# A diffusion layer on one core: products of the down-projection added up in PSUM, half sums on VectorE, a reordered end

## The chip, the cores and the metric

The kernel runs on one core of a Trainium2 chip. A core has five engines that matter here: TensorE (PE, with its weight loads PEld), VectorE (DVE), ScalarE (ACT), GpSimd (POOL) and SyncE (SP, which issues the DMAs). Each works through its own list of instructions in order and waits for others by semaphores. The metric is device time in microseconds, the median of three runs: 1337.65 us (1335.8 to 1337.68).

## The reference

One layer of a diffusion backbone over 1024 latent tokens and 256 context tokens, width 1024, all in float32: a token mixer (linear recurrence beside attention), then a gated convolution FFN with 2816 hidden channels, each wrapped in norms and modulation. The part that matters here is the last matmul of the FFN and what stands behind it:

```
def conv_ffn(h, w_up, conv_w, conv_b, w_down):
    up = dwconv(h @ w_up, conv_w, conv_b, FFN_CONV_LEFT)
    u, g = up[..., :D_FF], up[..., D_FF:]
    return (jax.nn.silu(g) * u) @ w_down
...
        x = x + gt2 * rms_norm(f_l, g_post_ffn[l])
```

`silu(g) * u` is called act here: 2816 channels by 1024 tokens. The down-projection is act (as 1024 x 2816) times w_down (2816 x 1024).

## The kernel before

The kernel is one long program for one core; in this part the order of every engine's work is the order of the code. The up-projection comes first; its results go through the convolution and the gate and into a buffer in DRAM, act_d, in 22 pages of 128 channels.

The down-projection, from 1100 us on, uses seven block products in place of eight. Both matrices are cut in halves along the 2816 channels (11 blocks of 128 each, NK = 11), act also into its left and right 512 tokens, w_down into its left and right 512 columns. A page of 128 x 1024 holds in its left half (lh) a piece of act and in its right half (rh) a piece of w_down; `ld` loads four kinds of page, blk[1] to blk[4]. A product n, numbered 1 to 7, works for each of its 11 blocks j on such a page or on one whose halves are sums of two pages' halves. `sums` makes these half sums (128 x 512 each), `prep` cuts the page into a high part (ScalarE's copy to the narrower float32r) and a low part (VectorE's difference, through the helper `lo`, line 76), and `dn` multiplies: for four tiles t of 128 tokens, three matmuls high x high, high x low, low x high, each 128 x 128 by 128 x 512.

A product and a block make a slot, 66 slots for the first six products in ORDER. In slot s the code issues the matmuls of s, the half sums for slot s + 4 and the parts for slot s + 3. Every product sums its 11 blocks in four PSUM banks of its own (`bank` hands out eight in turn), and `dn_out` takes the banks out in the first four slots of the following product: a copy on ScalarE or an add on VectorE into the result pages yt[0] to yt[7]. `dn_sums` adds pages once more. GpSimd does one half sum in each block of products 7, 5, 6, 3 and 4, VectorE the other one in products 7, 5 and 6.

Product 2 comes last and in three parts: tiles 0 and 1 together, then tile 2, then tile 3. The upper result pages yt[4] to yt[7] are complete before it and are finished beside it, by `fin`: a square with a row sum on ScalarE, the product with the row gt2, one over the root of the mean by a chain of small instructions (`rstd_of`, lines 101 to 106), then a scaling and addition on VectorE (line 1640) and the store. Pages yt[0] to yt[3] wait for product 2; `fin_head` does the half of their work that can be done early.

Pages come from a list `free`, from which `take` takes the oldest and to which `give` returns; a page is only written when its last reader has ended.

Of the kernel before, what the change touches and what calls it, by code (L numbers as in the profile page):

```python
# [14 lines left out]
D = 1024  # L15
# [6 lines left out]
EPS = 1e-6  # L22
# [12 lines left out]
def hybrid_layer_kernel(ctx: ExitStack, tc: tile.TileContext, A, out):  # L35
    nc = tc.nc
    V, S, G, T = nc.vector, nc.scalar, nc.gpsimd, nc.tensor
# [233 lines left out]
    junk = C([128, 384], mybir.dt.bfloat16)  # L271
# [77 lines left out]
    for n in range(4, 16):  # L349
        b, kp = order[n]  # L350
# [345 lines left out]
    for k in range(2):  # L696
# [3 lines left out]
        h_, l_ = L(F32R), L(F32R)  # L700
# [621 lines left out]
    free = []  # L1322

    def take(dt=F32R):
        k = free.pop(0)
        return {"L": L, "W": W, "F": Fp}[k](dt), k

    def give(*pages):
        free.extend(k for _, k in pages)

    blk = {c: {} for c in (1, 2, 3, 4)}
    opd = {}
    sm = {}
    dpo = {}
    yt = {}

# [6 lines left out]
        for e in es:  # L1343
            nc.sync.dma_start(out=blk[c][j][0][:, rh if e else lh], in_=(A["w_dn"] if e else act_d)[r:r + 128, x])

    def tt(e, o, a, b, op):
        (V if e == "v" else G).tensor_tensor(o, a, b, op)

    def sums(n, j):

        b = {c: blk[c][j][0] for c in blk if j in blk[c]}
        if n == 5:
            tt("g", b[2][:, lh], b[2][:, lh], b[3][:, lh], ALU.add)
            tt("v", b[2][:, rh], b[2][:, rh], b[1][:, rh], ALU.subtract)
        elif n == 6:
            tt("g", b[2][:, lh], b[2][:, lh], b[1][:, lh], ALU.subtract)
            tt("v", b[2][:, rh], b[3][:, rh], b[2][:, rh], ALU.subtract)
            give(blk[1].pop(j))
        elif n == 7:
            x = sm[j] = take(F32)  # L1360
            tt("g", x[0][:, lh], b[1][:, lh], b[2][:, lh], ALU.subtract)
            tt("v", x[0][:, rh], b[3][:, rh], b[2][:, rh], ALU.subtract)
        elif n == 3:
            tt("g", b[2][:, lh], b[4][:, lh], b[2][:, lh], ALU.subtract)
        elif n == 4:
            tt("g", b[2][:, rh], b[2][:, rh], b[4][:, rh], ALU.subtract)

    def prep(n, j):

        hi, l_ = take(), take()  # L1370
        if n in (3, 4):
            for p, x in ((blk[2][j], lh), (blk[3][j], rh)) if n == 3 else ((blk[3][j], lh), (blk[2][j], rh)):
                S.activation(hi[0][:, x], p[0][:, x], AF.Copy)
                lo("v", l_[0][:, x], p[0][:, x], hi[0][:, x])
        else:
            src = sm[j] if n == 7 else blk[{1: 1, 5: 2, 6: 2, 2: 4}[n]][j]
            S.activation(hi[0], src[0], AF.Copy)
            lo("v", l_[0], src[0], hi[0])
        if n == 7:
            give(sm.pop(j))  # L1380
        elif n == 2:
            give(blk[4].pop(j))
        elif n == 4:
            give(blk[2].pop(j), blk[3].pop(j))
        opd[n, j] = hi, l_

    def dn(n, j, ts=(0, 1, 2, 3)):
        hi, l_ = opd[n, j][0][0], opd[n, j][1][0]
        for t in ts:
            if j == 0:  # L1390
                dpo[n, t] = bank(t % 2)
            po = dpo[n, t]
            c = slice(t * 128, (t + 1) * 128)
            T.matmul(po, hi[:, c], hi[:, rh], start=j == 0, stop=False)
            T.matmul(po, hi[:, c], l_[:, rh], start=False, stop=False)  # L1395
            T.matmul(po, l_[:, c], hi[:, rh], start=False, stop=j == NK - 1)
        if 3 in ts:
            give(*opd.pop((n, j)))

    def dn_out(n, t):  # L1400

        po = dpo.pop((n, t))
        if n == 1:
            yt[t] = take(F32)[0]
        if n == 7:
            yt[4 + t] = take(F32)[0]
        y0, y1 = yt[t], yt.get(4 + t)
        if n in (1, 7, 5):
            S.activation(y0[:, lh] if n == 1 else y1[:, lh] if n == 7 else y1[:, rh], po, AF.Copy)
        elif n == 6:  # L1410
            V.tensor_tensor(y0[:, rh], po, y0[:, lh], ALU.add)
        elif n == 3:
            V.tensor_tensor(y0[:, rh], po, y0[:, rh], ALU.add)
        elif n == 4:
            V.tensor_tensor(y1[:, lh], y1[:, lh], po, ALU.subtract)
        else:
            V.tensor_tensor(y0[:, lh], po, y0[:, lh], ALU.add)  # L1417

    def dn_sums(t, q):

        y0, y1 = yt[t], yt[4 + t]
        if q == 0:
            G.tensor_tensor(y1[:, lh], y1[:, lh], y0[:, rh], ALU.add)
            V.tensor_tensor(y0[:, rh], y0[:, rh], y1[:, rh], ALU.add)
        else:
            G.tensor_tensor(y1[:, rh], y1[:, rh], y1[:, lh], ALU.add)

    with tc.manual_schedule():

# [149 lines left out]
            xo[i] = take(F32)[0]  # L1579
            nc.sync.dma_start(out=xo[i], in_=x1_d[i * 128:(i + 1) * 128, :])  # L1580

        ORDER = (1, 7, 5, 6, 3, 4, 2)
        slots = [(n, j) for n in ORDER[:-1] for j in range(NK)]
        preps = [(n, j) for n in ORDER[:-1] for j in range(NK)][3:]
        preps2 = list(range(NK))
        for s_, (n, j) in enumerate(slots):
            q = s_ // NK
            dn(n, j)
            if q and j < 4:
                dn_out(ORDER[q - 1], j)  # L1590
            if n == 1:
                if tail:
                    tail.pop(0)()
                for k in (2 * j, 2 * j + 1) if j < 4 else (j + 4,) if j < 7 else ():
                    ld(2, k)
                    ld(3, k, (1,))
            elif n == 7:
                ld(3, j, (0,))
            elif n == 6:
                ld(4, j)  # L1600
            elif n == 3:
                if 1 <= j < 5:
                    dn_sums(j - 1, 0)
                elif 5 <= j < 9:
                    dn_sums(j - 5, 1)
# [11 lines left out]
        ssf, rsf, epf = C([128, 8]), C([128, 8]), C([128, 8])
        yg = {}

        def fin_head(i):  # L1620


            c = slice(i, i + 1)
            yg[i] = take(F32)[0]
            S.activation(yg[i][:, rh], yt[i][:, rh], AF.Square, accum_out=ssf[:, c])
            V.tensor_scalar(out=epf[:, c], in0=ssf[:, c], scalar1=1.0 / D, scalar2=EPS, op0=ALU.mult, op1=ALU.add)
            G.tensor_tensor(yg[i][:, rh], yt[i][:, rh], gt2[:, rh], ALU.mult)

        def fin(i):

            c = slice(i, i + 1)
            a = lh if i < 4 else slice(0, D)
            if i >= 4:
                yg[i] = take(F32)[0]
            junk, k = take(F32)
            S.activation(junk[:, a], yt[i][:, a], AF.Square, accum_out=ssf[:, c])  # L1636
            (V if i < 4 else G).tensor_tensor(yg[i][:, a], yt[i][:, a], gt2[:, a], ALU.mult)
            rstd_of(rsf[:, c], ssf[:, c], 1, 1.0 / D, epf[:, c] if i < 4 else EPS)
            for a in (lh, rh):
                V.scalar_tensor_tensor(out=xo[i][:, a], in0=yg[i][:, a], scalar=rsf[:, c], in1=xo[i][:, a], op0=ALU.mult, op1=ALU.add)  # L1640
                nc.sync.dma_start(out=out[i * 128:(i + 1) * 128, a], in_=xo[i][:, a])
            free.append(k)

        for j in range(NK):
            dn(2, j, (0, 1))
            if preps2:
                prep(2, preps2.pop(0))
            if j < 4:
                x1_load(j)
                dn_out(4, j)  # L1650
            if j >= 3 and j < 11 and j % 2:
                fin(4 + (j - 3) // 2)
            elif j >= 3 and j < 11:
                fin_head((j - 4) // 2)
        dn_out(2, 0)
        fin(0)
        for j in range(NK):
            dn(2, j, (2,))
        dn_out(2, 1)
        fin(1)  # L1660
        for j in range(NK):
            dn(2, j, (3,))
        for t in (2, 3):
            dn_out(2, t)
            fin(t)
    pe_ctx.close()
    pe_r.close()

# [86 lines left out]
```

## Time and profile before

| what | value |
|---|---|
| median of the runs | 1337.65 us |
| profiled execution | 1337.59 us, span 1335.70 us |
| TensorE busy | 1279.3 us (96%) |
| VectorE busy | 1059.3 us (79%) |
| ScalarE busy | 730.3 us (55%) |
| GpSimd busy | 524.3 us (39%) |
| mean granted TensorE clock | 0.986 of full |
| down-projection, first to last matmul start | 1100.47 to 1321.23 us |

The span runs from the first to the last instruction. A row of a timeline gives when an instruction (or xN merged ones) started and how long it shows; neighbouring instructions on an engine overlap a little, so the step from one start to the next is shorter than what a row shows. Matmuls are pipelined: one shows 0.39 us, but the next starts after less.

### The profile page before, as it was taken

To read this page: it belongs to the slowest core of one execution; us is meant where nothing else is said; L and a number is where in the kernel's file an instruction comes from. 1 tells how busy PE (TensorE), PEld (TensorE's weight loads), DVE (VectorE), ACT (ScalarE), POOL (GpSimd) and SP (SyncE) were. 2 spreads that over 40 slices of the span, in tenths; PEclk is the share of its full clock that TensorE was granted. 3 is DMA by queue.
4 is the path that set the end of the run, shared out by engine and by line. 5 is a ranking of instruction groups with operands and counts; after the bars stand their busy time and mean duration, and the time that the engine had idled before them with its cause. 6 is when DMAs were issued, how large, how long until landed. Compare 5 with 4: busy or idle time off the path is not lost. (4 is left out here: it accounts for less than half of the span.)

```text
span 1335.7 us, 18049 instructions
## 1 busy us (share of the span) xinstructions
PE 1279.3 (96%) x6490; PEld 1049.6 (79%) x6490; DVE 1059.3 (79%) x1633; ACT 730.3 (55%) x1366; POOL 524.3 (39%) x441
## 2 busy tenths in 40 slices
PE   5999999799999999999998999999999999999895
PEld 3796666687999999888776888888888888878684
DVE  3654677768898988847589888887778779998998
ACT  4533785458999999934355433344334435334362
POOL 2410000215666666723042344423442324873922
PEclk8999999899999999999998999999999999999998
DMA  9533244000000001333321222222222368031033
GB/s 372 197 111 127 86 143 130 12 1 1 1 1 1 1 1 49 111 126 140 129 95 48 95 95 86 72 79 95 91 68 78 111 204 316 1 110 64 16 137 115
DMA packets 42184, 124.21 MB, mean 93 GB/s; under 512 B 4696, under 2 KB 4976, under 8 KB 42096
## 3 DMA queue, kind: packets, MB, share of 16 engines
q1 hardware_dynamic: 42096, 123.07, 26.2%
q8 instruction: 51, 0.84, 0.3%
q14 instruction: 37, 0.30, 0.1%
HBM read 101.02 MB, written 22.03 MB: 92 GB/s over the span
## 5 line engine op out<-in xcount | busy, mean ns | idle before, releaser
L1217 PE MATMUL b<-l,f 128*128 128x512 f32 x620 | 242.6, 391 | 5.6 <-DVE f L76 5.6
L1216 PE MATMUL b<-l,f 128*128 128x512 f32 x620 | 242.9, 392 | 3.9 <-DVE l L76 3.8
L1215 PE MATMUL b<-l,f 128*128 128x512 f32 x620 | 242.4, 391 | 0.5 <-issue 0.5
L1217 PEld LDWEIGHTS b<-l,f 128*128 128x128 f32 x620 | 117.0, 189 | 30.7 <-DVE f L76 6.4
L1216 PEld LDWEIGHTS b<-l,f 128*128 128x128 f32 x620 | 116.9, 189 | 30.5 <-DVE l L76 6.5
L906 POOL TENSOR_SCALAR r<-r,c 128x512 f32<-128x512 f32 (+1 forms) x128 | 100.9, 800 | 97.2 <-DVE c L901 68.2
L1215 PEld LDWEIGHTS b<-l,f 128*128 128x128 f32 x620 | 117.0, 189 | 25.2 <-issue 0.7
L1190 ACT ACTIVATE f<-w 128x1024 fp32r<-128x1024 f32 x21 | 22.3, 1060 | 198.8 <-POOL w L1187 198.8
L883 DVE TENSOR_REDUCE c<-s 128x1 f32<-128x512 f32 (+1 forms) x192 | 108.6, 594 | 25.6 <-PE s L880 24.1
L76 DVE TENSOR_TENSOR f<-w,f 128x1024 fp32r<-128x1024 f32 (+1 forms) x89 | 97.1, 1093 | 33.9 <-ACT f L1190 32.9
L1274 DVE SCALAR_TENSOR_TENSOR l<-f,c,l 128x1023 f32<-128x1023 f32 x88 | 123.4, 1403 | 0.7
L894 ACT ACTIVATE r<-s,c 128x512 f32<-128x512 f32 (+1 forms) x192 | 117.5, 620 | 6.2 <-DVE c L901 4.7
L1184 POOL TENSOR_TENSOR w<-w 128x512 f32<-128x512 f32 x21 | 27.9, 1328 | 230.7 <-DVE f L76 230.7
L76 DVE TENSOR_TENSOR l<-t,l 128x512 fp32r<-128x512 f32 x128 | 81.5, 678 | 1.4 <-ACT l L69 1.2
L914 PE MATMUL t<-c,r 128*128 128x128 f32 x640 | 81.7, 273 | 0.9 <-DVE r L76 0.6
L69 ACT ACTIVATE l<-t 128x512 fp32r<-128x512 f32 x128 | 69.4, 595 | 8.5 <-PE t L914 7.7
L1268 ACT ACTIVATE l<-f,c 128x1024 f32<-128x1024 f32 x44 | 54.5, 1238 | 34.9 <-DVE f L1255 34.4
L914 PEld LDWEIGHTS t<-c,r 128*128 128x128 f32 x640 | 71.3, 140 | 2.6 <-PE t L914 0.8
L878 PE MATMUL s<-r,w 96*128 96x512 f32 (+1 forms) x192 | 69.5, 362 | 1.0 <-ACT r L894 0.7
L1063 PE MATMUL po<-l,r 128*128 128x512 f32 x256 | 69.3, 390 | 0.0
L938 PE MATMUL o<-l,r 128*128 128x256 f32 x256 | 68.7, 301 | 0.0
L879 PE MATMUL s<-r,w 96*128 96x512 f32 (+1 forms) x192 | 68.6, 358 | 0.0
(376 smaller groups left out, 3318.2 us busy)
## 6 DMA issues: line engine op xcount, KB each, us to landing
w<-in_w_up SPq DMA_DIRECT2D x44, 512.0 KB
r<-in_w_mod SPq DMA_DIRECT2D x32, 512.0 KB
act<-l SPq DMA_DIRECT2D x22, 512.0 KB
l<-in_w_m SPq DMA_DIRECT2D x16, 512.0 KB
l<-act SPq DMA_DIRECT2D x30, 256.0 KB
l<-in_w_dn SPq DMA_DIRECT2D x30, 256.0 KB
w<-in_w_fm SPq DMA_DIRECT2D x8, 512.0 KB
w<-in_w_out SPq DMA_DIRECT2D x8, 512.0 KB
```

The lines of the kernel that those rows point to most:

```text
L69: S.activation(o, i, AF.Copy)
L76: return (V if e == "v" else G).tensor_tensor(o, src, f(hi), ALU.subtract)
L878: T.matmul(ps[:, :n], qh[0:96, q], kh[0:96, a:a + n], start=True, stop=False)
L883: V.tensor_reduce(out=stat[:, i % 4, c:c + 1], in_=sc[i, c][:, :CK[c][1]], op=ALU.min, axis=AX.X)
L894: S.activation(pt_[i][:, a:a + n], sc.pop((i, c))[:, :n], AF.Exp, scale=-1.0, bias=st[:, 3:4], accum_out=st[:, 4 + c:5 + c])
L906: G.tensor_scalar(out=p[:, a:a + n], in0=p[:, a:a + n], scalar1=stat[:, i % 4, 7:8], scalar2=1.0, op0=ALU.mult, op1=ALU.mult)
L914: T.transpose(ps[:, c, :], pt_[i][:, (c0 + c) * 128:(c0 + c + 1) * 128], ident)
L1063: T.matmul(po[:, n * 512:(n + 1) * 512], w, wo[k][0][:, n * 512:(n + 1) * 512], start=st, stop=en)
L1215: T.matmul(po, wh, bh, start=k == 0 and b == wb[0][1], stop=False)
L1216: T.matmul(po, wh, bl, start=False, stop=False)
L1217: T.matmul(po, wl, bh, start=False, stop=k == 3 and b == wb[-1][1])
L1274: V.scalar_tensor_tensor(out=x[:, a], in0=x0[:, b], scalar=P("fcw", j * 3 + k, 1), in1=x[:, a], op0=ALU.mult, op1=ALU.add)
```

## The change

Products that belong to the same result are added up in the same PSUM banks. The order of products becomes 1, 7, 6, 5, 3, 4, 2. Products 1, 6, 5 and 3 share four banks (chain "a"): 6, 5 and 3 begin without the start flag, so their matmuls add to what stands there, and after each of the four products ScalarE copies the banks out, tile by tile within the last slot of the product. Products 7 and 4 share the other four (chain "b"), with 4's sign carried by its operands. `dn_sums` goes. All half sums are done by VectorE, in place in the pages, so product 7 needs no page of its own. At the end the squares are split in halves, those of the right halves done during product 4; GpSimd multiplies the upper pages and the right halves of the lower pages by gt2 in place; the small chains run once for four pages, once for two and twice for one; and the scalings are instructions of full width, but for the last two pages.

```diff
-        if n == 5:
-            tt("g", b[2][:, lh], b[2][:, lh], b[3][:, lh], ALU.add)
-            tt("v", b[2][:, rh], b[2][:, rh], b[1][:, rh], ALU.subtract)
...
+        o, x, y, op = {7: (2, 1, 2, (ALU.subtract, None)), 6: (2, 3, 2, (ALU.subtract, None)), 5: (1, 2, 1, (ALU.add, None)),
+                       3: (2, 4, 2, (ALU.subtract, None)), 4: (2, 4, 2, (None, ALU.subtract))}.get(n, (0, 0, 0, (None, None)))
+        if op[0]:
+            V.tensor_tensor(b[o][:, lh], b[x][:, lh], b[y][:, lh], op[0])
+        if n == 6:
+            V.tensor_tensor(b[2][:, rh], b[1][:, rh], b[2][:, rh], ALU.add)
+        elif n in (5, 7):
+            V.tensor_tensor(b[o][:, rh], b[3][:, rh], b[2][:, rh], ALU.subtract)
...
+    CHAIN = {1: "a", 6: "a", 5: "a", 3: "a", 7: "b", 4: "b", 2: "c"}
...
+        sk = n in (6, 5, 3, 4)
+        st = j == 0 and not sk
...
+            T.matmul(po, hi[:, c], hi[:, rh], start=st, stop=False, skip_group_check=sk)
...
+    def dn_7(t):
+
+        y = yt[4 + t][:, rh]
+        V.tensor_tensor(y, dpo["b", t], y, ALU.add)
...
-        ORDER = (1, 7, 5, 6, 3, 4, 2)
+        ORDER = (1, 7, 6, 5, 3, 4, 2)
...
-            dn(n, j)
-            if q and j < 4:
-                dn_out(ORDER[q - 1], j)
+            for t in range(4):
+                dn(n, j, (t,))
+                if j == NK - 1 and n in (1, 6, 5, 3):
+                    dn_out(n, t)
...
+            if n == 4 and j > 2:
+                square(j - 3, rh, ssf, jk)
...
+        def times_gt(e, i, a):
+            e.tensor_tensor(yt[i][:, a], yt[i][:, a], gt2[:, a], ALU.mult)
+
+        def rstd(a, n):
+            c = slice(a, a + n)
+            V.tensor_tensor(ssl[:, c], ssl[:, c], ssf[:, c], ALU.add)
+            rstd_of(rsf[:, c], ssl[:, c], n, 1.0 / D)
+
+        def fin(i, parts=(slice(0, D),)):
+
+            for a in parts:
+                V.scalar_tensor_tensor(out=xo[i][:, a], in0=yt[i][:, a], scalar=rsf[:, i:i + 1], in1=xo[i][:, a], op0=ALU.mult, op1=ALU.add)
+                nc.sync.dma_start(out=out[i * 128:(i + 1) * 128, a], in_=xo[i][:, a])
...
+                square(4 + j, lh, ssl, jk)
+                times_gt(G, 4 + j, slice(0, D))
+            if j == 4:
+                rstd(4, 4)
+            if 4 <= j < 8:
+                times_gt(G, j - 4, rh)
+                fin(j)
+        for t in (0, 1):
+            dn_out(2, t)
+            square(t, lh, ssl, jk)
+        for t in (0, 1):
+            times_gt(V, t, lh)
+        rstd(0, 2)
...
+        for t in (0, 1):
+            fin(t)
         for t in (2, 3):
+            if t == 3:
+                for j in range(NK):
+                    dn(2, j, (3,))
             dn_out(2, t)
+            square(t, lh, ssl, jk)
+            times_gt(V, t, lh)
+            rstd(t, 1)
+            fin(t, (lh, rh))
```

VectorE in the middle of product 7, before. Line 1347 is a half sum, line 76 the low part; the names are pages with their numbers (l, f and w are three pools of pages), what is written first.

```order
L1347 TENSOR_TENSOR l_10508<-l_10276,l_10273 128x512
L76 TENSOR_TENSOR l_10512<-l_10486,l_10511 128x1024
L1347 TENSOR_TENSOR f_10528<-f_10299,f_10296 128x512
L76 TENSOR_TENSOR f_10532<-l_10508,f_10531 128x1024
L1347 TENSOR_TENSOR l_10548<-l_10320,l_10317 128x512
```

The same place now; lines 1351 and 1355 are the two half sums.

```order
L1355 TENSOR_TENSOR f_10299<-f_10302,f_10299 128x512
L76 TENSOR_TENSOR f_10526<-l_10276,f_10525 128x1024
L1351 TENSOR_TENSOR l_10320<-l_10069,l_10320 128x512
L1355 TENSOR_TENSOR l_10320<-l_10323,l_10320 128x512
L76 TENSOR_TENSOR f_10545<-f_10299,l_10544 128x1024
```

One half sum per slot stood here, the other on GpSimd; now both stand here, and each writes into a page that it reads.

VectorE at the very end, before: the last tile is picked up from PSUM (line 1417), multiplied by gt2 (line 1637), and after the small steps scaled (line 1640, two instructions).

```order
L1417 TENSOR_TENSOR f_10505<-b_11803,f_10505 128x512
L1637 TENSOR_TENSOR l_11735<-f_10505,l_11403 128x512
L101 TENSOR_SCALAR rs_11856<-c_11576,c_11578 128x1
L103 RECIPROCAL c_11577<-rs_11856 128x1
L104 TENSOR_TENSOR rs_11856<-c_11577 128x1
L105 SCALAR_TENSOR_TENSOR rs_11856<-rs_11856 128x1
L106 SCALAR_TENSOR_TENSOR c_11577<-rs_11856,c_11577 128x1
L1640 SCALAR_TENSOR_TENSOR f_11618<-l_11735,c_11577,f_11618 128x512 x2
```

And now:

```order
L1412 TENSOR_TENSOR f_10422<-b_11728,f_10422 128x512
L1614 TENSOR_TENSOR f_10422<-f_10422,w_11368 128x512
L1618 TENSOR_TENSOR c_10167<-c_10167,c_10166 128x1
L101 TENSOR_SCALAR rs_11766<-c_10167 128x1
L103 RECIPROCAL c_10168<-rs_11766 128x1
L104 TENSOR_TENSOR rs_11766<-c_10168 128x1
L105 SCALAR_TENSOR_TENSOR rs_11766<-rs_11766 128x1
L106 SCALAR_TENSOR_TENSOR c_10168<-rs_11766,c_10168 128x1
L1624 SCALAR_TENSOR_TENSOR f_11594<-f_10422,c_10168,f_11594 128x512 x2
```

The product with gt2 (line 1614) now writes the page that it reads, which is also the page that ScalarE squares, and one small add (line 1618) is new.

## Rows read from the trace of the kernel before

**Rows 1.** Busy time by stretch: bounds, length, each engine (instructions), clock, DMA share, GB/s.
```profile
core 0: us, PE busy (x) PEld busy (x) DVE busy (x) ACT busy (x) POOL busy (x), PEclk, DMA share, GB/s
...
1162.00:1193.00 31.00, 29.06 (x124) 22.53 (x123) 31.00 (x19) 10.53 (x11) 25.82 (x14) 1.00 0.29 101
...
1321.00:1336.00 15.00, 0.62 (x3) 0.19 (x1) 10.08 (x26) 2.78 (x9) 0.00 (x0) 0.66 0.35 130
```
**Rows 2.** Timeline of TensorE: start, us shown, engine, line, operation, out<-in, idle before.
```profile
1100.25 0.39 PE L1217 MATMUL b<-l,f 128*128 128x512 f32 x1
1100.47 0.39 PE L1394 MATMUL b<-f 128*128 128x512 f32 x1
...
1130.39 0.39 PE L1394 MATMUL b<-f 128*128 128x512 f32 x1
...
1246.08 0.50 PE L1395 MATMUL b<-l,l 128*128 128x512 f32 x1 [2.01 <-DVE l L76]
...
1306.50 0.39 PE L1394 MATMUL b<-l 128*128 128x512 f32 x1
...
1321.23 0.39 PE L1396 MATMUL b<-l,l 128*128 128x512 f32 x1
```
**Rows 3.** Waits from 1096 us on: who for whom, us in total, times, longest.
```profile
PEld b L1395 <- DVE l L76: 6.1, 9, 2.4
...
PE b L1395 <- DVE l L76: 2.8, 3, 2.0
```
**Rows 4.** Busy time in the stretch behind the longest wait, columns as in rows 1.
```profile
1246.40:1250.80 4.40, 4.40 (x14) 3.46 (x13) 4.40 (x3) 1.90 (x4) 4.40 (x4) 0.61 0.00 0
```
**Rows 5.** Timeline of GpSimd.
```profile
1133.72 1.67 POOL L1347 TENSOR_TENSOR l<-l,l 128x512 f32<-128x512 f32 x1 [2.90 <-DVE f L76]
...
1145.72 15.78 POOL L1347 TENSOR_TENSOR l<-l,l 128x512 f32<-128x512 f32 x8
...
1293.24 2.41 POOL L1637 TENSOR_TENSOR l<-f,l 128x1024 f32<-128x1024 f32 x1 [23.99 <-issue]
```
**Rows 6.** Timeline of VectorE in product 7.
```profile
1131.83 0.68 DVE L1347 TENSOR_TENSOR f<-l,l 128x512 f32<-128x512 f32 x1
1132.43 1.21 DVE L76 TENSOR_TENSOR f<-l,f 128x1024 fp32r<-128x1024 f32 x1
...
1150.70 1.77 DVE L1347 TENSOR_TENSOR l<-l,w 128x512 f32<-128x512 f32 x1
1152.40 2.31 DVE L76 TENSOR_TENSOR l<-l,f 128x1024 fp32r<-128x1024 f32 x1
```
**Rows 7.** Timeline of ScalarE: a high part, then a copy out of a bank.
```profile
1160.44 1.06 ACT L1377 ACTIVATE f<-l 128x1024 fp32r<-128x1024 f32 x1 [1.37 <-DVE l L1347]
1161.41 0.58 ACT L1409 ACTIVATE f<-b 128x512 f32<-128x512 f32 x1
```
**Rows 8.** Timeline of VectorE and ScalarE: a pick from PSUM, and the last chain.
```profile
1100.67 0.69 DVE L1258 TENSOR_TENSOR f<-b,f 128x512 f32<-128x512 f32 x1 [2.03 <-PE b L1217]
...
1328.59 0.68 DVE L1417 TENSOR_TENSOR f<-b,f 128x512 f32<-128x512 f32 x1
1329.31 0.69 DVE L1637 TENSOR_TENSOR l<-f,l 128x512 f32<-128x512 f32 x1
1329.36 0.63 ACT L1636 ACTIVATE l<-f 128x512 f32<-128x512 f32 x1 [2.92 <-DVE f L1417]
...
1330.12 0.21 DVE L101 TENSOR_SCALAR rs<-c,c 128x1 f32<-128x1 f32 x1
...
1331.38 1.41 DVE L1640 SCALAR_TENSOR_TENSOR f<-l,c,f 128x512 f32<-128x512 f32 x2
```
**Rows 9.** Timeline of ScalarE and VectorE in product 2: table load, scaling, first pick.
```profile
1294.37 1.28 ACT L102 ACT_TABLE_LOAD   x1
...
1296.75 4.45 DVE L1640 SCALAR_TENSOR_TENSOR l<-l,c,l 128x512 f32<-128x512 f32 x2
...
1316.20 0.68 DVE L1417 TENSOR_TENSOR f<-b,f 128x512 f32<-128x512 f32 x1
```

More of the change, by code (lines that the diff above doesn't have):

```diff
@@ L1332, in hybrid_layer_kernel @@
     opd = {}
-    sm = {}
     dpo = {}
@@ L1344, in ld @@
             nc.sync.dma_start(out=blk[c][j][0][:, rh if e else lh], in_=(A["w_dn"] if e else act_d)[r:r + 128, x])
-    def tt(e, o, a, b, op):
-        (V if e == "v" else G).tensor_tensor(o, a, b, op)
     def sums(n, j):
         b = {c: blk[c][j][0] for c in blk if j in blk[c]}
-        if n == 5:
-            tt("g", b[2][:, lh], b[2][:, lh], b[3][:, lh], ALU.add)
-            tt("v", b[2][:, rh], b[2][:, rh], b[1][:, rh], ALU.subtract)
[L1355 to L1364, printed above, removed]
+        o, x, y, op = {7: (2, 1, 2, (ALU.subtract, None)), 6: (2, 3, 2, (ALU.subtract, None)), 5: (1, 2, 1, (ALU.add, None)),
[6 more added lines that the diff above has]
+            V.tensor_tensor(b[o][:, rh], b[3][:, rh], b[2][:, rh], ALU.subtract)
         elif n == 4:
-            tt("g", b[2][:, rh], b[2][:, rh], b[4][:, rh], ALU.subtract)
+            V.tensor_tensor(b[2][:, rh], b[4][:, rh], b[2][:, rh], ALU.subtract)
     def prep(n, j):
@@ L1375, in prep @@
         else:
-            src = sm[j] if n == 7 else blk[{1: 1, 5: 2, 6: 2, 2: 4}[n]][j]
+            src = blk[{1: 1, 7: 2, 6: 2, 5: 1, 2: 4}[n]][j]
             S.activation(hi[0], src[0], AF.Copy)
             lo("v", l_[0], src[0], hi[0])
-        if n == 7:
-            give(sm.pop(j))
+        if n == 5:
+            give(blk[1].pop(j))
         elif n == 2:
@@ L1385, in prep @@
         opd[n, j] = hi, l_
+    CHAIN = {1: "a", 6: "a", 5: "a", 3: "a", 7: "b", 4: "b", 2: "c"}
     def dn(n, j, ts=(0, 1, 2, 3)):
         hi, l_ = opd[n, j][0][0], opd[n, j][1][0]
+        sk = n in (6, 5, 3, 4)
+        st = j == 0 and not sk
         for t in ts:
-            if j == 0:
-                dpo[n, t] = bank(t % 2)
-            po = dpo[n, t]
+            if st:
+                dpo[CHAIN[n], t] = bank(t % 2)
+            po = dpo[CHAIN[n], t]
             c = slice(t * 128, (t + 1) * 128)
-            T.matmul(po, hi[:, c], hi[:, rh], start=j == 0, stop=False)
-            T.matmul(po, hi[:, c], l_[:, rh], start=False, stop=False)
-            T.matmul(po, l_[:, c], hi[:, rh], start=False, stop=j == NK - 1)
+            T.matmul(po, hi[:, c], hi[:, rh], start=st, stop=False, skip_group_check=sk)
+            T.matmul(po, hi[:, c], l_[:, rh], start=False, stop=False, skip_group_check=sk)
+            T.matmul(po, l_[:, c], hi[:, rh], start=False, stop=j == NK - 1, skip_group_check=sk)
         if 3 in ts:
@@ L1400, in dn_out @@
     def dn_out(n, t):
-        po = dpo.pop((n, t))
+        po = dpo[CHAIN[n], t]
         if n == 1:
             yt[t] = take(F32)[0]
-        if n == 7:
+            S.activation(yt[t][:, lh], po, AF.Copy)
+        elif n == 6:
             yt[4 + t] = take(F32)[0]
[L1407 to L1411, printed above, removed]
+            S.activation(yt[4 + t][:, lh], po, AF.Copy)
+        elif n == 5:
+            S.activation(yt[4 + t][:, rh], po, AF.Copy)
         elif n == 3:
-            V.tensor_tensor(y0[:, rh], po, y0[:, rh], ALU.add)
-        elif n == 4:
-            V.tensor_tensor(y1[:, lh], y1[:, lh], po, ALU.subtract)
-        else:
[L1417 to L1426, printed above, removed]
+            S.activation(yt[t][:, rh], po, AF.Copy)
+        else:
+            y = yt[4 + t] if n == 4 else yt[t]
+            V.tensor_tensor(y[:, lh], po, y[:, lh], ALU.add)
+    def dn_7(t):
+        y = yt[4 + t][:, rh]
+        V.tensor_tensor(y, dpo["b", t], y, ALU.add)
     with tc.manual_schedule():
@@ L1585, in hybrid_layer_kernel, with square @@
         preps2 = list(range(NK))
+        ssf, ssl, rsf = C([128, 8]), C([128, 8]), C([128, 8])
+        def square(i, a, acc, page):
+            S.activation(page[0][:, a], yt[i][:, a], AF.Square, accum_out=acc[:, i:i + 1])
         for s_, (n, j) in enumerate(slots):
-            q = s_ // NK
-            dn(n, j)
-            if q and j < 4:
-                dn_out(ORDER[q - 1], j)
+            for t in range(4):
+                dn(n, j, (t,))
+                if j == NK - 1 and n in (1, 6, 5, 3):
+                    dn_out(n, t)
             if n == 1:
@@ L1598, in hybrid_layer_kernel @@
                 ld(3, j, (0,))
-            elif n == 6:
+            elif n == 5:
                 ld(4, j)
[L1601 to L1605, printed above, removed]
+            elif n == 3 and 1 <= j < 5:
+                dn_7(j - 1)
             if preps:
@@ L1615, in hybrid_layer_kernel @@
                 gt2 = gt_row(1, take(F32)[0])
[L1617 to L1640, printed above, removed]
+                jk = take(F32)
+            if n == 4 and j > 2:
[9 more added lines that the diff above has]
+                V.scalar_tensor_tensor(out=xo[i][:, a], in0=yt[i][:, a], scalar=rsf[:, i:i + 1], in1=xo[i][:, a], op0=ALU.mult, op1=ALU.add)
                 nc.sync.dma_start(out=out[i * 128:(i + 1) * 128, a], in_=xo[i][:, a])
-            free.append(k)
         for j in range(NK):
@@ L1650, in hybrid_layer_kernel @@
                 dn_out(4, j)
[L1651 to L1656, printed above, removed]
+                square(4 + j, lh, ssl, jk)
[11 more added lines that the diff above has]
+        rstd(0, 2)
         for j in range(NK):
             dn(2, j, (2,))
[L1659 to L1662, printed above, removed]
+        for t in (0, 1):
+            fin(t)
         for t in (2, 3):
+            if t == 3:
+                for j in range(NK):
+                    dn(2, j, (3,))
             dn_out(2, t)
-            fin(t)
+            square(t, lh, ssl, jk)
+            times_gt(V, t, lh)
+            rstd(t, 1)
+            fin(t, (lh, rh))
     pe_ctx.close()
```

## The prediction

> **What bounds the kernel now.** I read the stages first, then the engine that waits, then what slowed the engine it waits for. In the table by stage [rows 1] TensorE is busy 29.06 of 31 us in a stretch of the down-projection in which VectorE is busy all 31; after 1321 us TensorE has 3 matmuls left and VectorE works on for 10 us. So there are two places to look at: TensorE's stalls from 1100 to 1321 us, and the 14 us behind its last matmul.
>
> The stalls. 132 matmuls, one product, start between 1100.47 and 1130.39 [rows 2]: 29.92 / 132 = 0.2267 us each with nothing in the way. The down-projection has 7 products x 11 blocks x 4 tiles x 3 = 924 matmuls, 923 steps from the first start to the last: 209.2 us at that pace. The last starts at 1321.23, which is 220.8 us after the first. **11.5 us are lost.** The list of waits [rows 3] names one releaser: VectorE's line 76, which makes the low part of the operands. The rows of TensorE and of its weight loads overlap, so I take the loss from the starts and only the cause from this list. Part of the loss is a lower clock: the longest wait is 2.01 us, up to 1246.08 [rows 2], and in 4.4 us behind it the granted clock is 0.61 of full [rows 4], a mix of its levels of 1.2 and 2.4 GHz.
>
> Why VectorE is late. GpSimd's half sums run without a gap from 1145.72 for 15.78 us, 8 of them [rows 5]; in that time the rows of VectorE's line 76 and of its own half sum show 2.31 and 1.77 us. GpSimd's row at 1133.72 stands behind 2.90 us of idleness [rows 5], and in that gap the same two show 1.21 and 0.68 [rows 6]. From start to start a row takes some 0.07 less than it shows (1131.83 to 1132.43 is 0.60, 1150.70 to 1152.40 is 1.70), so I count 2.23 and 1.70 beside GpSimd, 1.14 and 0.60 alone. So each half sum on GpSimd costs VectorE 1.10 us of waiting, though VectorE could do it in 0.60. One block (a slot) takes TensorE 12 x 0.2267 = 2.72 us; VectorE needs 2.23 + 1.70 = 3.93 where two GpSimd sums meet its pair, and 2.23 + 0.60 = 2.83 where one does. Both are above 2.72, and that is the stall.
>
> The Trainium skill, SBUF — State Buffer, section on the two separate sides, calls the port pair of the two engines an exclusive lock, held for a whole instruction; by that rule a GpSimd sum costs VectorE its whole duration, and the trace agrees (1.10 us more beside each).
>
> **The sums moved to VectorE.** Before, GpSimd did 55 half sums (one per block for products 7, 5, 6, 3 and 4), VectorE 33. Now VectorE does all 88. A slot of products 7, 6 and 5 costs it 1.14 + 2 x 0.60 = 2.34 us against 2.72: 0.38 to spare where it was 0.1 to 1.2 short. Products 3 and 4 need one half sum and two half-width low parts, which I put at 0.60 each, like a half sum: 1.80. While product 4 runs, the low part for product 2 comes on top: 2.94, 0.22 too much in seven slots, 1.5 us, which the lead of three slots (8.2 us) covers. GpSimd has no instruction left before product 2, so nothing takes the cover away. Stalls that go: 11.5 us; the next that could be late is ScalarE, whose 1.06 + 0.58 us per slot [rows 7] stay far below 2.72. The loads of the blocks, of gt2 and of x1 stay in the same slots on SP; outputs leave in 10 transfers in place of 16, the last two unchanged.
>
> **Adding up in PSUM.** This puts a new wait at two joins, 6 to 5 and 5 to 3: the first matmul of a tile may only add to its bank when ScalarE has read it. (1 to 7, 7 to 6, 3 to 4 and 4 to 2 use banks read long before.) TensorE comes back to the bank ten starts after the tile's last matmul: 2.27 us. A reader starts 0.42 us after that matmul's start (1100.25 to 1100.67 [rows 2, 8]) and takes 0.58, so the bank is free after 1.00, or 2.06 when a 1.06 us activation stands in front. Later tiles arrive 0.68 apart and are read 0.58 apart. I take 0. From above: if the reads come only when the whole product has ended, each join waits 1.0 us, with two activations in front 3.1, and with the slow clock of rows 4 some 1 more: 2 to 8 us for both. What queues behind a waiting read on ScalarE are the high parts, needed three slots later. The output sums at the joins shrink: 12 VectorE adds of 0.60 in place of 20, 16 ScalarE copies in place of 12, no GpSimd ones in place of 8. All lie beside matmuls and cost nothing while VectorE has its 0.38 per slot.
>
> **The end.** Before, product 2's first two tiles, done when the third began at 1306.50 [rows 2], were only picked up from 1316.20 on [rows 9], because VectorE's two-part scalings for the upper rows took 4.45 us each (three of four; beside GpSimd [rows 9]) where alone such a pair takes 1.41 [rows 8]. From there the four finishing chains ran one behind the other and TensorE's end did not matter: 1335.70 − 1321.23 = 14.5 us.
>
> Now TensorE's starts are: product 2 at 1100.47 + 792 x 0.2267 = 1280.0, third tile at 1295.0, fourth at 1302.5, last matmul 1309.7. VectorE: four picks at 0.60 up to 1282; four half-width squares on ScalarE (0.76 each [rows 8]) to 1283; table load, root and small steps, 1294.37 to 1296.75 before [rows 9], to 1285.4. Four full-width scalings of about 1.3 wait for GpSimd's four full products (2.41 each alone [rows 5]), which alternate with them: 1281.5 + 4 x (2.41 + 1.3) = 1296.3. Picks of tiles 0 and 1 to 1297.5, squares 1298.3, their two products beside GpSimd's last four (1.70 each) to about 1301, small steps 1302.5, two scalings 1305.3. The pick of tile 2 (ready at 1302.9) starts there, and its chain, the terms below up to the scaling of 1.41, 5.1 us, ends at 1310.4. The last pick can start at 1309.7 + 0.42 = 1310.1. So VectorE comes 0.3 late, at 1310.4, with nothing to spare.
>
> The last chain, from the rows of the last one before [rows 8]: pick to square 0.77, square to its sum 0.76, the in-place product 0.69 (before it ran beside the square; now it must wait for it, as both use one tile), one more small add, put at 0.21 like line 101, the small steps 1330.12 to 1331.38 = 1.26, then from the scaling to the end of the span 1335.70 − 1331.38 = 4.32. Sum 8.01. End of the span: 1310.4 + 8.0 = 1318.4.
>
> **Sum.** The stalls give 11.5 us, the end 14.5 − (1318.4 − 1309.7) = 5.8 us: 17.3 in all. The profiled execution took 1337.59 us, 1.89 more than its span of 1335.70, and is within 0.1 us of the median of the runs, 1337.65. 1337.6 − 17.3 = **1320.3 us**. Its own range is 1317.5 to 1322.5.
>
> **The rivals.**
> A late end: VectorE misses TensorE's last matmul because the four scalings take 4.45 us each as before: 1285.4 + 17.8 = 1303.2, then tiles 0 and 1 as above 9 us to 1312.2, tile 2 5.1 to 1317.3, and 8.01 for tile 3: 1325.3 + 1.9 = 1327.2. For it: my timetable has no slack. Against: the full-width GpSimd products now start 12 us earlier and are no longer woven between the scalings one for one.
> Waits at the two joins: 2 to 8 us, middle 4: 1324. For it: ScalarE is in order, and the high parts stand in front. Against: 0.2 us of slack even then.
> The stalls stay and only change their name (pages, ScalarE, DMA): only the end gains, 1331.8. For it: the operand pages are few. Against: every wait of TensorE in rows 3 is VectorE's, and in the first product, where VectorE kept up, there is none.
> Slower: VectorE's 2.23 and 1.70 us are not GpSimd's doing but belong to two-input work on this memory under load, so the slots of products 7, 6 and 5 become 2.23 + 2 x 0.60 = 3.43 at least. 33 x (3.43 − 2.72) = 23.4 us of stall for 11.5, less 5.8 at the end: 1337.6 + 11.9 − 5.8 = 1343.7. It decides from a slot of 2.72 + 17.3 / 33 = 3.24 us on. For it: half of VectorE's rows show such times. Against: rows 5 and 6 have them only while GpSimd runs. The Trainium skill, Perfetto Trace Analysis, section on optimizing Scalar/DVE operations, takes this side as far as it says that a saturated VectorE may shed work to GpSimd (this change does the reverse); it then doubts the gain for the shared port, and the rows bear out the doubt.
> That the change does not do what it says would show as GpSimd sums left in products 7 to 4; the order of its instructions has none.
>
> **How the numbers follow.** Forecast 0.64, late end 0.12, joins 0.08, stalls that stay 0.08, slower 0.06, the rest near no change 0.02. The range of 1317 to 1328 holds the forecast, the late end and the joins. A difference within 0.2% (2.7 us) counts as no change, being about what this measurement can tell. Faster 0.92, same 0.02, slower 0.06.
>
> **What would show it.** In the profile of the changed kernel line 76 should take 1.21 us everywhere from 1131 us to product 2, no matmul of lines 1391 to 1393 should wait for VectorE, and the last one should start near 1309.7. A gap of TensorE at the start of products 5 or 3 released by ScalarE would show the joins wrong. Behind the start of the last matmul about 8.7 us should remain; more than 10 means that VectorE came late. Low parts of 2.3 us with GpSimd idle would overturn the whole argument.

## The result, and the profile after

The changed kernel takes 1320.2 us (median of 4 runs, 1317.91 to 1321.15); the kernel before took 1337.54 on the same chip (4 runs, 1335.8 to 1337.68). The ratio is 0.9871, 95% interval [0.9854, 0.9888]: faster by 1.3%, at the forecast of 1320.3, inside its range. The profiled execution took 1321.15 us, with a span of 1319.3.

The profile is compared from the first matmul of the down-projection to the end of the span, because its start differs between the runs of this case (1098.93 to 1101.37 us) for reasons that lie ahead of it. I call this the stage. Before it was 1335.70 − 1100.47 = 235.2 us, now 1319.3 − 1100.75 = 218.55: 16.7 less, where 17.3 had been forecast.

The table by stage, of the changed kernel, columns as in [rows 1]; the first line has the bounds of the first line there, the second begins with the last matmul:

```profile
1162.00:1193.00 31.00, 31.00 (x138) 25.67 (x137) 22.73 (x30) 12.58 (x14) 0.00 (x0) 1.00 0.08 29
1310.00:1319.30 9.30, 0.35 (x2) 0.00 (x0) 4.69 (x12) 0.93 (x3) 0.00 (x0) 0.63 0.30 113
```

In 31 us TensorE now starts 138 matmuls instead of 124 and has no idle time; VectorE, with twice the number of half sums, is busy 22.73 us instead of 31.00. GpSimd is the column that went from 25.82 to nothing. Behind the last matmul 9.3 us are left instead of 14.5.

TensorE's timeline, first and last matmul of the down-projection, as in [rows 2]:

```profile
1100.75 0.39 PE L1391 MATMUL b<-f 128*128 128x512 f32 x1
...
1309.97 0.39 PE L1393 MATMUL b<-f,l 128*128 128x512 f32 x1
```

That is 209.22 us for 923 steps, the 0.2267 us of an undisturbed step throughout. The list of waits, which had VectorE's line 76 at its head [rows 3], is empty for TensorE and its weight loads from 1100 to 1320 us.

VectorE's timeline in product 7, where [rows 6] had 1.77 and 2.31:

```profile
1149.97 0.68 DVE L1351 TENSOR_TENSOR l<-l,l 128x512 f32<-128x512 f32 x1
1150.58 0.68 DVE L1353 TENSOR_TENSOR l<-w,l 128x512 f32<-128x512 f32 x1
1151.18 1.22 DVE L76 TENSOR_TENSOR l<-f,l 128x1024 fp32r<-128x1024 f32 x1
1152.31 0.69 DVE L1351 TENSOR_TENSOR l<-l,l 128x512 f32<-128x512 f32 x1
```

Two half sums and a low part take 1152.31 − 1149.97 = 2.34 us, as worked out.

The end did not go by the timetable. GpSimd's products with gt2 in the changed kernel:

```profile
1280.77 9.47 POOL L1614 TENSOR_TENSOR f<-f,w 128x1024 f32<-128x1024 f32 x4 [202.68 <-ACT l L1580]
1290.20 4.76 POOL L1614 TENSOR_TENSOR l<-l,w 128x512 f32<-128x512 f32 x3
1294.93 2.27 POOL L1614 TENSOR_TENSOR f<-f,w 128x512 f32<-128x512 f32 x1
```

And VectorE beside them and after them, to the last scaling (lines 1618 and 101 to 106 are the small steps, 1624 the scalings, 1412 the picks from PSUM):

```profile
1283.24 2.32 DVE L101 TENSOR_SCALAR rs<-c 128x4 f32<-128x4 f32 x1
1285.83 0.18 DVE L103 RECIPROCAL c<-rs 128x4 f32<-128x4 f32 x1 [0.27 <-ACT rs L102]
1286.04 1.87 DVE L104 TENSOR_TENSOR rs<-c 128x4 f32<-128x4 f32 x1
1287.94 2.32 DVE L105 SCALAR_TENSOR_TENSOR rs<-rs 128x4 f32<-128x4 f32 x1
1290.30 1.22 DVE L106 SCALAR_TENSOR_TENSOR c<-rs,c 128x4 f32<-128x4 f32 x1
1291.61 2.21 DVE L1624 SCALAR_TENSOR_TENSOR l<-f,c,l 128x1024 f32<-128x1024 f32 x1
...
1299.40 1.27 DVE L1412 TENSOR_TENSOR l<-b,l 128x512 f32<-128x512 f32 x2
1300.93 1.45 DVE L1614 TENSOR_TENSOR l<-l,w 128x512 f32<-128x512 f32 x2 [0.25 <-ACT l L1580]
...
1302.48 0.17 DVE L101 TENSOR_SCALAR rs<-c 128x2 f32<-128x2 f32 x1
...
1306.17 0.68 DVE L1412 TENSOR_TENSOR l<-b,l 128x512 f32<-128x512 f32 x1
...
1311.04 0.68 DVE L1412 TENSOR_TENSOR f<-b,f 128x512 f32<-128x512 f32 x1
1312.57 0.69 DVE L1614 TENSOR_TENSOR f<-f,w 128x512 f32<-128x512 f32 x1 [0.85 <-ACT l L1580]
...
1314.57 1.41 DVE L1624 SCALAR_TENSOR_TENSOR f<-f,c,f 128x512 f32<-128x512 f32 x2
```

Four of the small steps for the upper rows, on 128 x 4 numbers, show 1.22 to 2.32 us; the same line 101 on 128 x 2 takes 0.17 once GpSimd is done. Taken with GpSimd's rows, the cause can be read off: GpSimd's four full products end every 9.47 / 4 = 2.37 us, at 1283.1, 1285.5, 1287.9 and 1290.2, and three of the long steps end at 1285.56, 1287.91 and 1290.26, a few hundredths behind such an end. Small as they are, these steps wait until GpSimd's instruction is over. So the scalings start at 1291.61, 6.2 us later than forecast.

### The profile page after: what moved, and what is told of

It is laid out like the page before. It is cut to its first block, busy times and chain, and to the rows that moved or that the text cites. A ratio compares the mean times of both kernels' runs of the same rounds, so it can differ in the third digit from the quotient of the medians.

```text
span 1319.3 us, 17942 instructions
## 1 busy us (share of the span) xinstructions
PE 1273.5 (97%) x6490; PEld 1049.8 (80%) x6490; DVE 1019.7 (77%) x1654; ACT 733.3 (56%) x1374; POOL 410.3 (31%) x378
## 4 chain that ended last, share of the span: by engine, by line
PE 80%; DVE 11%; ACT 5%; issue 2%; DMA 2%; SPq 0%; POOL 0%; DVEq 0%; ACTq 0%; POOLq 0%
PE b L1217 10%; PE b L1215 10%; PE b L1216 10%; PE t L914 5%; PE po L1063 4%; PE b L1392 4%; PE b L1391 4%; PE b L1393 4%; DVE l L76 3%; PE s L878 3%; PE o L939 3%; PE o L938 3%; PE s L879 3%; PE s L880 2%; PE po L1066 2%
## 5 line engine op out<-in xcount | busy, mean ns | idle before, releaser
L1614 POOL TENSOR_TENSOR f<-f,w 128x1024 f32<-128x1024 f32 (+1 forms) x5 | 11.7, 2372 | 202.7 <-ACT l L1580 202.7
```

## The experiments

All stages below are measured as above; 218.55 us is that of the changed kernel in its first profile, and 218.6 in a second one.

**The sums alone.** The kernel before, with all its half sums on VectorE, through the helper that makes them:

```diff
-        (V if e == "v" else G).tensor_tensor(o, a, b, op)
+        V.tensor_tensor(o, a, b, op)
```

> The kernel before with one edit: all its half sums on VectorE; order of products, PSUM banks and end as before. If GpSimd's sums slowed VectorE and VectorE stalled TensorE, the 11.5 us of stalls go and the rest stays: the last matmul starts near 1309.7 us, the end stays 14 to 15 us long because its chains run one behind the other on VectorE, and the time is 1337.5 - 11.5 = about 1326 us. If adding up in PSUM is what freed TensorE, the time stays near 1337. If VectorE is slow by itself, its 33 to 88 half sums make it 1340 or more.

Measured: 1324.92 us against 1338.37 (0.9906 [0.9891, 0.9921]), at the forecast of the theory. In the profile TensorE's first to last start is 211.6 us, 2.4 more than without a stall, and the stage is 223.8. So 9.2 of the 11.5 us of stalls went. The stage gained 2.2 us more at the end, which the expectation had left as it was: 12.2 us behind the last matmul in place of 14.5. VectorE, whose chains set the end in this program, begins its first scaling 184.9 us after the first matmul (1286.31 − 1101.37), 11.3 us earlier than before (1296.75 − 1100.47 = 196.3), and from that scaling to the end of the span both take 38.9 us. What is left of the stalls lies in product 3. Timelines of VectorE and of GpSimd there:

```profile
1234.43 3.48 DVE L76 TENSOR_TENSOR f<-l,l 128x512 fp32r<-128x512 f32 x2
...
1243.03 1.28 DVE L76 TENSOR_TENSOR f<-f,f 128x512 fp32r<-128x512 f32 x2
```
```profile
1233.92 3.44 POOL L1426 TENSOR_TENSOR f<-f 128x512 f32<-128x512 f32 x2
```

Line 1426 belongs to `dn_sums`, the output sums that this version still has on GpSimd. Two low parts beside them take 3.48 us, and 1.28 when GpSimd is idle. So the loss follows GpSimd, not the kind of work on VectorE: this rules out the rival in which VectorE is slow by itself, and the one in which the stalls stay.

**All but the sums.** The changed kernel with 55 half sums given back to GpSimd, one per block as before:

```diff
-            V.tensor_tensor(b[o][:, lh], b[x][:, lh], b[y][:, lh], op[0])
+            G.tensor_tensor(b[o][:, lh], b[x][:, lh], b[y][:, lh], op[0])
...
-            V.tensor_tensor(b[2][:, rh], b[4][:, rh], b[2][:, rh], ALU.subtract)
+            G.tensor_tensor(b[2][:, rh], b[4][:, rh], b[2][:, rh], ALU.subtract)
```

> The changed kernel with the left half sums of products 7, 6, 5 and 3 and the right ones of product 4 back on GpSimd (55 of 88); the rest unchanged. If the sums are the cause, VectorE loses 55 x (1.10 - 0.60) = 27 us of its room again, low parts of 2.3 us return, TensorE stalls some 8 to 12 us and the time is 1328 to 1332 us. If adding up in PSUM is the cause, it stays at 1320.

Measured: 1328.65 us (0.9931 [0.9916, 0.9946]), as the theory has it. VectorE's timeline and the list of TensorE's waits (for whom, us in total, times, longest) show the picture of before, in a program whose products add up in PSUM:

```profile
1163.27 1.77 DVE L1353 TENSOR_TENSOR l<-w,l 128x512 f32<-128x512 f32 x1
1164.97 2.32 DVE L76 TENSOR_TENSOR f<-l,f 128x1024 fp32r<-128x1024 f32 x1
```
```profile
PE b L1392 <- DVE f L76: 2.7, 4, 0.9
```

Each part alone gives less than the whole (0.94% and 0.69%, together 1.3%). TensorE's first to last start is 217.8 us: it loses 8.5 us here, not 11.5, presumably because the other edits had already taken some GpSimd work out of the stage (not tested by itself).

**The price of one meeting.** The changed kernel with one GpSimd sum more per slot in products 7, 6 and 5, into a tile that nothing reads any more; VectorE's work is untouched:

```diff
...
+            if n in (7, 6, 5):
+                G.tensor_tensor(spare, f(hi[0])[:, lh], f(hi[0])[:, lh], ALU.add)
```

> The changed kernel with one more GpSimd instruction in each slot of products 7, 6 and 5, a sum of 128 x 512 whose two inputs are the high part just made and whose result nobody reads: 33 of them. If each holds VectorE up for its length, VectorE's slot is 2.34 + 1.10 = 3.44 us against TensorE's 2.72: up to 33 x 0.72 = 24 us of stall, less the lead of 8, so the last matmul starts 15 to 24 us later and the time is 1335 to 1344 us. If GpSimd does not slow VectorE, it stays at 1320.

Measured: 1332.87 us in one run, stage 230.4: slower by 12, the direction of the theory, some 2 us short of its range. VectorE's timeline through a slot, and GpSimd's:

```profile
1181.00 1.21 DVE L76 TENSOR_TENSOR f<-l,l 128x1024 fp32r<-128x1024 f32 x1
1182.13 0.68 DVE L1351 TENSOR_TENSOR f<-f,f 128x512 f32<-128x512 f32 x1
1182.74 1.52 DVE L1353 TENSOR_TENSOR f<-l,f 128x512 f32<-128x512 f32 x1
1184.18 1.21 DVE L76 TENSOR_TENSOR f<-l,f 128x1024 fp32r<-128x1024 f32 x1
```
```profile
1182.39 1.32 POOL L1372 TENSOR_TENSOR c<-f 128x512 f32<-128x512 f32 x1 [1.87 <-ACT f L1370]
```

Only the VectorE instruction that meets it pays: 1.52 instead of 0.68, 0.84 us, and the slot takes 1184.18 − 1181.00 = 3.18 us instead of 2.34. GpSimd's row began 0.35 us before that instruction did, beside the one in front of it. Another of its rows tells what it did in that time:

```profile
1217.70 1.04 POOL L1372 TENSOR_TENSOR c<-w 128x512 f32<-128x512 f32 x1 [2.15 <-ACT w L1370]
```

This one begins just as VectorE goes from its first sum to its second (1217.76) and shows 1.04 us, and the second sum shows 1.53 as elsewhere. So the 0.3 us more of the other rows were waiting for the sum in front, and the price of 0.84 is most of the 1.04 that the GpSimd sum takes, but below the 1.10 per sum of the prediction.

**GpSimd busy, but reading nothing.** In the same place a fill with zeros, released in the same way by a one-column copy on ScalarE:

```diff
...
+            if n in (7, 6, 5):
+                S.activation(mark, spare[:, 0:1], AF.Copy)
+                G.memset(spare, 0.0)
```

> The same with a GpSimd instruction that only writes (it sets a 128 x 512 tile to zero), paced by a 128 x 1 copy on ScalarE. If any GpSimd instruction takes the pair from VectorE, low parts show 1.6 to 2.3 us again and the time is above 1325 us. If only one that reads does, as the Trainium skill, SBUF — State Buffer, section on the two separate sides, has it for VectorE instructions with two inputs, the low parts stay at 1.21 us and the time at 1320.

Measured: 1320.81 us in one run, stage 218.6, no gap of TensorE. The timelines of VectorE and GpSimd have them side by side:

```profile
1142.91 0.69 DVE L1355 TENSOR_TENSOR f<-f,f 128x512 f32<-128x512 f32 x1
```
```profile
1142.56 0.53 POOL L1374 MEMSET c<- 128x512 f32 x1 [1.87 <-ACT c L1373]
```

GpSimd runs until 1143.09, into VectorE's sum, and the sum takes its 0.69. From 1131 to 1225 us, beside 31 such fills, every group of VectorE's low parts and half sums has the mean that it has without them, 1.21 to 1.22 and 0.68 to 0.69 us. So it is not GpSimd being at work that holds VectorE: a fill, which reads nothing, does not, and a sum with two operands does. The Trainium skill, SBUF — State Buffer, section on the two separate sides, says this of a VectorE instruction with two SBUF inputs: it is blocked only by a GpSimd instruction that reads SBUF. The run agrees.

**Slower reads at the joins.** ScalarE copies the banks out four times over after products 6 and 5:

```diff
-            S.activation(yt[4 + t][:, lh], po, AF.Copy)
+            for _ in range(4):
+                S.activation(yt[4 + t][:, lh], po, AF.Copy)
```

(and the same for the other half of the page.)

> The changed kernel with ScalarE's copies out of the shared banks after products 6 and 5 done four times each, so that the banks come free late. If the next product's first matmul on a bank waits for the last read, bank k is free 0.42 + 2.2 (k + 1) us after tile 0's last matmul, TensorE comes to it at 2.27 + 0.68 k: it waits 0.35 us for the first and 4.9 us in all, at each of the joins 6 to 5 and 5 to 3 and nowhere else, released by ScalarE: 1320 + 9.8 = 1330 us, 1 or 2 more if the clock falls. If the joins have far more room than I counted, it stays at 1320.

Measured: 1336.47 us in one run, stage 234.6: 16 us lost, where 10 to 12 had been expected. TensorE's timeline at the first join, and ScalarE's:

```profile
1190.53 0.50 PE L1391 MATMUL b<-f 128*128 128x512 f32 x1 [0.54 <-ACT f L1406]
...
1192.91 0.50 PE L1391 MATMUL b<-f 128*128 128x512 f32 x1 [1.41 <-ACT f L1406]
...
1195.29 0.59 PE L1391 MATMUL b<-f 128*128 128x512 f32 x1 [1.42 <-ACT f L1406]
...
1197.66 0.79 PE L1391 MATMUL b<-f 128*128 128x512 f32 x1 [0.93 <-ACT f L1406]
```
```profile
1187.99 9.62 ACT L1406 ACTIVATE f<-b 128x512 f32<-128x512 f32 x16 [8.18 <-PE b L1393]
```

A copy takes 9.62 / 16 = 0.60 us, and the first matmul of each tile waits for four of them. The idle times of the rows add up to 4.3 us here and 4.1 at the second join, but they leave out that a row shows 0.39 us where a step is 0.2267. By the starts, the fourth tile begins at 1197.66, 10.09 us after the first tile's last matmul (1187.57), where 19 steps take 4.31: 5.8 us late at this join and as much at the next, for the 4.9 of the expectation, which had a copy at 0.55. The rest of the loss, 16.0 − 2 × 5.8 = 4.4 us, is the clock, from the table by stage behind the first join:

```profile
1187.00:1195.60 8.60, 5.23 (x21) 3.41 (x20) 0.00 (x0) 7.32 (x13) 0.00 (x0) 1.00 0.39 122
1195.60:1202.40 6.80, 5.87 (x14) 4.10 (x13) 3.81 (x5) 4.86 (x7) 0.00 (x0) 0.50 0.23 77
```

Behind a stretch in which TensorE was busy 5.23 of 8.60 us the granted clock is 0.50, the lower of its levels (1.2 GHz), for 6.8 us, in which 14 matmuls start where 30 would at full pace; part of that is the last wait, and behind it the steps are 0.43 us. So a join that does not fit costs more than its waits, here 8.0 us, of which 2.2 for the clock. In the changed kernel the same place is this, TensorE's timeline and ScalarE's:

```profile
1188.25 0.39 PE L1393 MATMUL b<-l,f 128*128 128x512 f32 x1
...
1190.51 0.39 PE L1391 MATMUL b<-f 128*128 128x512 f32 x1
```
```profile
1188.67 2.64 ACT L1405 ACTIVATE f<-b 128x512 f32<-128x512 f32 x4 [8.18 <-PE b L1393]
```

The first read starts 0.42 us behind the tile's last matmul and ends some 0.6 later, at 1189.3; product 5 wants the bank at 1190.51. The joins have 1.2 us to spare.

**The end without GpSimd.** All products with gt2 at the end on VectorE:

```diff
-                times_gt(G, 4 + j, slice(0, D))
+                times_gt(V, 4 + j, slice(0, D))
...
-                times_gt(G, j - 4, rh)
+                times_gt(V, j - 4, rh)
```

> The changed kernel with the end's eight products with gt2 on VectorE in place of GpSimd, nothing else. If the lock between the two engines makes the small steps of line 101 to 106 take 1.2 to 2.3 us each and the scalings 2.2, both fall back to 0.2 and 1.2 us, VectorE's work for the upper pages ends near 1295 us in place of 1299.4, the last pick starts 0.42 us after the last matmul in place of 1.1, and the time is 0.7 us lower, 1319.5. If VectorE's own work counts for more than the lock, the upper pages end later than 1299.4 and the time is the same or up to 4 us longer.

Measured: 1320.64 us (0.9867 [0.9851, 0.9883]), stage 217.9, 0.65 less. VectorE's timeline:

```profile
1290.42 0.17 DVE L101 TENSOR_SCALAR rs<-c 128x4 f32<-128x4 f32 x1
...
1292.15 1.28 DVE L1624 SCALAR_TENSOR_TENSOR l<-f,c,l 128x1024 f32<-128x1024 f32 x1
...
1310.73 0.69 DVE L1412 TENSOR_TENSOR f<-b,f 128x512 f32<-128x512 f32 x1 [0.33 <-PE b L1393]
```

The same instruction, line 101 on 128 x 4, takes 0.17 where it took 2.32, and a scaling 1.28 where it took 2.21: the cause read above is shown. VectorE now does the eight products as well and still picks up the last tile on time, having waited for it. The scalings start only at 1292.15, though, because each product here stands behind a square of ScalarE's (0.85 us idle), and they end at 1298.8, not near 1295 as expected; and the gain is no more than the 0.65 us by which the last pick had been late. In the time of the runs that cannot be told from nothing.

**A shorter last chain.** The same with the last two tiles' products written into a page of their own, so that they run beside the square, and the small add folded into line 101:

```diff
...
-            times_gt(V, t, lh)
-            rstd(t, 1)
-            fin(t, (lh, rh))
+            yg = take(F32)[0]
+            V.tensor_tensor(yg[:, lh], yt[t][:, lh], gt2[:, lh], ALU.mult)
+            rstd_of(rsf[:, t:t + 1], ssl[:, t:t + 1], 1, 1.0 / D, epf[:, t:t + 1])
+            fin(t, (lh, rh), (yg, yt[t]))
```

> The changed kernel with the end's products with gt2 on VectorE, and for tiles 2 and 3 the product into a page of its own, beside the square, and the sum of the two half squares folded into line 101. The last chain is then that of before, 7.0 us from the pick to the end of the span in place of 8.2, and the pick is not late (0.7 us): 1319.3 - 1.9 = 1317.4 for the span, 0.14% below the changed kernel, against which it runs here. If the end is held by the output's transfer, it is no shorter than the changed kernel.

Measured: 1319.32 us (0.9861 [0.9847, 0.9876]), stage 217.0, and from the last pick to the end of the span 7.34 us (7.43 in a second profile), where 7.0 had been expected and the changed kernel has 8.26. VectorE's timeline (line 1659 is the product, now right behind the pick):

```profile
1309.37 0.69 DVE L1412 TENSOR_TENSOR f<-b,f 128x512 f32<-128x512 f32 x1 [1.01 <-PE b L1393]
1310.09 0.69 DVE L1659 TENSOR_TENSOR l<-f,w 128x512 f32<-128x512 f32 x1
```

The rows are from the second profile of this version. From the pick to the scaling it is now 2.80 us, 3.53 in the changed kernel: so the in-place product and the add cost 0.7 us, and the other 0.2 lie behind the scaling. The changed kernel, run again beside it, took 1319.97 us (0.9869 [0.9852, 0.9885]); its expectation was:

> The changed kernel once more, on the same chip as the short chain: 1320 us.

The stage shows a gain of 1.6 us for this edit and the one before it together; the times of the runs, whose intervals overlap, leave it open.

**The lesson tried elsewhere.** TensorE's waits for line 76 that remain lie in the up-projection, near 700 us, where GpSimd makes half sums too. The short-chain version with those on VectorE:

```diff
         def sums():
-            G.tensor_tensor(g[:, rh], g[:, lh], g[:, rh], ALU.add)
+            V.tensor_tensor(g[:, rh], g[:, lh], g[:, rh], ALU.add)
```

(and its three other lines alike.) The expectation counts the edit wrongly: it moves 84 instructions, 21 pairs of pages, of which 12 lie before 742 us, where TensorE waits; the other 72 lie beside matmuls that wait for nothing, in the base and in this version.

> The short-chain version, with the four half-width sums of each of the last three operand pairs of the up-projection (lines 1184 to 1187, twelve instructions) moved from GpSimd to VectorE. In the kernel after, TensorE stands still or runs slow for about 13 us between 664 and 740 us, and VectorE is busy 19.7 of 20 us there. Theory (a GpSimd sum holds VectorE 1.10 us, the same sum on VectorE itself takes 0.60): VectorE gets back 12 x 0.5 = 6 us, and the time falls by 3 to 6 us against the short-chain version of the same session, to about 1314 to 1316. Rival (the sums on GpSimd fell beside VectorE work that does not meet them, or the order on VectorE puts the twelve sums ahead of what TensorE waits for): no change within 1.5 us, or up to 4 us slower.

> The short-chain version once more, on the chip of the run before, as the base to compare it with: 1319 us, within 1.5 us.

Measured: 1315.8 us (1315.45 to 1315.99; 0.9833 [0.9819, 0.9848]) against 1319.24 (1318.53 to 1319.95; 0.9861 [0.9844, 0.9877]) for its base on the same chip: 3.4 us faster, the low end of the theory. In the profiles the down-projection begins 3.1 us earlier (1096.64 for 1099.73) and the stage is the same (217.0 and 217.1). TensorE's waits from 600 to 1100 us, of the base and then of this version:

```profile
PE b L1217 <- DVE f L76: 5.6, 2, 5.1
PE b L1216 <- DVE l L76: 3.8, 4, 1.3
```
```profile
PE b L1217 <- DVE f L76: 3.3, 3, 1.7
PE b L1216 <- DVE l L76: 3.3, 3, 1.3
PE b L1215 <- ACT f L1190: 1.5, 1, 1.5
```

The longest wait falls from 5.1 to 1.7 us, and the granted clock from 720 to 740 us rises from 0.83 to 1.00. VectorE is still busy 19.8 of 20 us there, so part of the waits stays. From 740 us to the down-projection VectorE is now busy 322.7 of 354 us (289.1 of 357 in the base), and TensorE all of it in both. This version beats both kernels: its interval lies below those of the changed kernel too ([0.9854, 0.9888] and [0.9852, 0.9885]).

## Why the prediction was right, point by point

**The stalls.** Right in size and cause: 11.5 us were to go, and TensorE's time from first to last start fell from 220.76 to 209.22. VectorE's slot of 2.34 us and the 1.21 us of its low parts came as written. That GpSimd's sums were the cause is shown by giving them back (8.5 us lost again), by moving them alone (all but 2.4 us gained, and those beside GpSimd work that was left), and by a GpSimd instruction that does nothing useful. The prediction's price of 1.10 us for each GpSimd sum was read where these sums run without a gap; for a single meeting it is too high: 0.84 us, of the 1.04 that the GpSimd sum takes. And its split into stalls and end is not one into the two edits: the sums moved alone also took 2.2 us off the end.

**The joins.** Right: nothing is waited for, and the 1.0 us to the free bank is what the rows show. The price that I gave for the rival (some 1 us of slow clock beside waits of 1.0 to 3.1) was not tried at that size; the quadrupled reads cost 2.2 us of it at each join, beside 5.8 us of late reads. The room rests on VectorE being on time, as the rival had it: with the additional GpSimd sums, a high part that had waited 2.10 us for VectorE stood on ScalarE before the reads of the first join. They began 2.7 us behind the tile's last matmul (1198.05 for 1195.34), and TensorE waited 0.89 us for ScalarE.

**The end.** Right in its sum by luck: two errors mostly cancel. The failed step is "table load, root and small steps, 1294.37 to 1296.75 before, to 1285.4". In that stretch one step alone met GpSimd's product (1293.24 to 1295.65 [rows 5]), line 101 in VectorE's timeline of the kernel before, and this one was not held:

```profile
1294.83 0.14 DVE L101 TENSOR_SCALAR rs<-c 128x1 f32<-128x1 f32 x1
```

The other steps came after 1295.65. Here line 101 works on 128 x 4, four of the five small instructions each waited for a GpSimd product, and the scalings began at 1291.61, 6.2 us late. I had applied the lock to wide instructions only. Half of this was made up at once: the scalings were to run in step with GpSimd's four full products, but those were over by 1290.24, and only half-width products stood beside the first scalings, so they ended 3.1 us late (1299.4 for 1296.3). Another 2.2 us came back, most of it because the products of tiles 0 and 1, put at 1.70 each beside GpSimd, now found it finished and took 1.45 for both: tile 2 was picked up at 1306.17 for 1305.3, and the last tile 0.65 us after it could have been, for 0.3. The last chain took 8.26 us for 8.01: 3.53 from the pick to the scaling for 3.69, and 4.73 from there to the end of the span for 4.32. Together 5.1 us instead of 5.8. The rival of the late end had its way in part: VectorE did miss the last matmul, by 0.65 us.

**The sum.** 16.7 us in the profile for 17.3. The medians differ by 17.3, but one execution scatters by more than the 0.6 between these, so that agreement says nothing more.

## What to carry to other kernels

Count what a GpSimd instruction with SBUF operands costs VectorE before giving work away: if VectorE can do it in less than it would wait, take it back, even from a VectorE that looks fully busy. This holds for tiny instructions too: most of the small steps here waited for as long as a wide one would. Keep GpSimd's work away from a chain of small steps that others wait for. A result may be added up in PSUM across products and read in between at no cost, if TensorE returns to a bank later than the read ends; if it does not, reckon with the clock as well as with the wait.

## What the hardware showed that I had not expected

- A VectorE instruction on 128 x 4 numbers took 2.32 us beside GpSimd's products and 0.17 without them, for one with a single tensor operand too (line 101). Not all small ones wait: the reciprocal, line 103, ran in 0.18 us in the middle of a GpSimd product (1285.83, between 1285.5 and 1287.9), and line 101 on 128 x 1 in 0.14 (1294.83, before). What separates them was not tested.
- A GpSimd fill of 128 x 512 took 0.53 us and held VectorE up by nothing.
- Some 4 us of idle time at a join were followed by 6.8 us at a granted clock of 0.50.
